# The choice of 256 keys in the 640-key block, moved from eight-at-a-time maxima to the shared bisection

## The chip, the cores and the metric

One core of a Trainium2 chip runs the whole kernel. The metric is the device time of one execution in microseconds (us). The engines are named as the profile names them: PE (TensorE's matrix products; PEld is its loading of weights), DVE (VectorE), ACT (ScalarE), POOL (GpSimd) and SP (SyncE, which issues the DMAs).

## What is computed

The kernel is one layer of a decoder over 1024 tokens of width 1024, in float32. Two token mixers work side by side on a common input projection: FoX, a causal softmax attention with a forget bias, and DSA, a sparse attention that lets each query see its 256 best keys only. Both have 8 heads of 64. Their outputs are gated, projected and normalised, and a SwiGLU block follows. The part that matters here is how DSA's keys are chosen, by an indexer's score:

```python
rel = jax.nn.relu(jnp.einsum('bqhd,bkd->bqhk', iqb, ik).astype(jnp.float32))
score = jnp.einsum('bqh,bqhk->bqk', iwb.astype(jnp.float32) * IDX_SCALE, rel)
score = jnp.where(kpos[None, None, :] <= qpos[None, :, None], score, NEG_INF)
_, idx = lax.top_k(score, topk)          # topk = 256
```

Queries come in blocks of 128. Block i may see 128*(i+1) keys, so blocks 0 and 1 need no choice, and blocks 2 to 7 choose 256 of 384, 512, 640, 768, 896 and 1024 keys.

## The kernel before

**Stages.** First the input is split into high and low parts (matrix products run as three products of such parts, `mm3`, lines 96 to 101), and the indexer's scores are made into six tiles `SM[2]` to `SM[7]`, [128 queries, 128*(i+1) keys] each (lines 242 to 284). Then comes the attention stage (lines 532 to 599): 64 steps, the first 32 for FoX and the last 32 for DSA. A step takes one head and one pair of query blocks, in the order of `ORDER = (3, 0, 2, 1)`. The mixing, the two normalisations and the feed-forward block follow, from line 600 on.

**One attention step.** `weigh` makes the scores of two query blocks on PE (lines 459 to 462). DVE takes the row maxima (line 469; for DSA's blocks with a choice line 472, which adds the mask `SM[i]` at the same time). ACT takes the exponentials (lines 470, 475), DVE the reciprocals (line 476), and POOL scales (line 479). `average` transposes the weights on PE (line 502), splits them on ACT and DVE (lines 503, 504) and multiplies with the values on PE (lines 511, 512). ACT and DVE put the result `o` together (lines 526, 527), which happens once in a step. Between these PE does `filler` work: projections for later heads, whose results ACT and DVE bring out of PSUM (lines 395, 396, 406, 407, 431, 432, 441), and gates (line 380).

**The choice of keys.** It is emitted at step `KSEL = 31` (lines 581 to 586), but its operands are ready much earlier. PE's order is written out by hand (`tc.manual_schedule`, line 564). A scheduler puts the instructions of the other engines in an order, and it draws the choice forward into FoX's steps. Once put in order, each engine works through its own list strictly in that order. There are two ways to choose:

- `select_by_max` (lines 287 to 292), on DVE alone: 32 times the eight greatest values are taken (`max`, line 290) and overwritten (`match_replace`, line 291); a last pass makes the mask (line 292). Before the change it serves the blocks of 384, 512 and 640 keys, one after the other.
- `select_by_bisection` (lines 294 to 361) finds the 256th greatest value bit by bit, for several blocks at once. In each of 32 counts ACT runs over every block's whole tile and counts by signs (line 310). DVE then makes of the counts, for all blocks together, the next bit and the next threshold in three tiny instructions (lines 311, 320, 318). ACT's next count waits for that threshold. After the loop DVE alone makes the last passes: two exact counts over each block (lines 333, 348), and for each piece of up to 512 keys a sequence of five passes that settles ties and writes the mask (lines 355 to 361). Before the change it serves the blocks of 768, 896 and 1024 keys.

```python
        def count(bias):
            for x, i in enumerate(blocks):
                j = at.tile([128, L], BF, name="junk", tag="junk", bufs=1)
                act.activation(j[:, :128 * (i + 1)], SM[i], AF.Sign, bias=bias(x), accum_out=s[:, x:x + 1])
            dve.tensor_tensor(a, s, thr, op=OP.is_ge)
```

The mask tiles are first read by DSA's steps (line 472).

Of the kernel before, what the change touches and what calls it, by code (L numbers as in the profile page):

```python
# [31 lines left out]
LAG = 2  # L32
W = (1, 1, 1, 1)
PW = 512
BIS = ((7, 6, 5),)
IDX_SCALE = (8 ** -0.5) * (64 ** -0.5)

NMM, NT = 2, 2
# [11 lines left out]
def trunk_kernel(ctx: ExitStack, tc: tile.TileContext, xT, xn, wt, wbr, wout, wfi, wfo,  # L50
# [236 lines left out]
    def select_by_max(i):  # L287
        for _ in range(TOPK // 8):
            m8 = mk.tile([128, 8], F32, name="m8", tag="m8", bufs=2)
            dve.max(m8, SM[i])  # L290
            dve.match_replace(SM[i], m8, SM[i], SENT)
        dve.tensor_scalar(SM[i], SM[i], SENT, -BIG, op0=OP.not_equal, op1=OP.mult)
# [280 lines left out]
    for k, (n, a, G) in enumerate(todo):  # L573
# [7 lines left out]
        if k == KSEL:  # L581
            for blocks in BIS:
                select_by_bisection(blocks, blocks[0])
            for i in range(2, 8):
                if not any(i in blocks for blocks in BIS):
                    select_by_max(i)
# [476 lines left out]
```

## Time and profile before

| | |
|---|---|
| median of 3 runs | 1687.06 us (1686.71 to 1687.7) |
| the profiled execution, its own time | 1685.55 us |
| the profiled execution, its span | 1683.6 us |
| PE busy | 1611.2 us, 96% of the span |
| PEld busy | 1314.1 us, 78% |
| DVE busy | 1186.1 us, 70% |
| ACT busy | 777.3 us, 46% |
| POOL busy | 673.3 us, 40% |

The span is the time from the first to the last instruction in the trace of the profiled execution; 1.95 us of its time lie around it. Busy times are those of one engine over the whole span. They are averages over stages of a very different kind, so what a change in one stage is worth has to be read from that stage: from the busy time of each engine in a stretch, and from what the waits in it end on.

### The profile page before, as it was taken

What the parts mean: (1) busy time and instruction counts of PE and PEld (TensorE: products, weight loads), DVE (VectorE), ACT (ScalarE), POOL (GpSimd) and SP (SyncE); (2) the same over time, 40 slices, a digit from 0 to 9 for tenths busy, and PEclk for the clock granted to TensorE, in tenths of its full rate; (3) what the DMA queues carried; (4) which work ended last, traced back from release to release, by engine and by line L of the source; (5) the groups of instructions that cost most, each with busy time, mean ns of one, the idle gap of its engine ahead of it and who ended that gap; (6) DMA issues with size and microseconds to landing.
All of it is one profiled execution on the core that took longest, in us unless ns stands there. A gap on an engine that the chain in (4) does not pass through costs nothing. (4 is left out here: it accounts for less than half of the span.)

```text
span 1683.6 us, 22519 instructions
## 1 busy us (share of the span) xinstructions
PE 1611.2 (96%) x7722; PEld 1314.1 (78%) x7722; DVE 1186.1 (70%) x2074; ACT 777.3 (46%) x1374; POOL 673.3 (40%) x652
## 2 busy tenths in 40 slices
PE   7998999998999999999999999999899999999997
PEld 5776887776788888888778877877677888888886
DVE  5889999979645454544775569776778766567776
ACT  6777878884444445544431034222123333253341
POOL 1122333332333333332441136434345555377673
PEclk9999999999999999999999999999899999999999
DMA  5112212121122222223865123565554333398552
GB/s 176 48 40 65 60 45 59 57 70 43 57 66 63 70 58 71 61 65 126 270 208 194 50 88 102 190 203 184 172 180 139 107 101 107 132 329 309 179 169 105
DMA packets 96379, 202.83 MB, mean 120 GB/s; under 512 B 10820, under 2 KB 37444, under 8 KB 96264
## 3 DMA queue, kind: packets, MB, share of 16 engines
q1 hardware_dynamic: 96264, 201.39, 36.6%
q8 instruction: 61, 1.00, 0.3%
q14 instruction: 54, 0.44, 0.1%
HBM read 139.40 MB, written 53.03 MB: 114 GB/s over the span
## 5 line engine op out<-in xcount | busy, mean ns | idle before, releaser
L99 PE MATMUL mm<-xh,whi 128*128 128x512 f32 (+1 forms) x720 | 296.0, 411 | 16.2 <-ACT whi L147 6.4
L101 PE MATMUL mm<-xl,whi 128*128 128x512 f32 (+1 forms) x720 | 281.4, 391 | 1.1 <-DVE xl L157 1.0
L100 PE MATMUL mm<-xh,wlo 128*128 128x512 f32 (+1 forms) x720 | 280.7, 390 | 0.5 <-DVE wlo L148 0.5
L479 POOL TENSOR_SCALAR p<-p,st 128x512 f32<-128x512 f32 (+1 forms) x192 | 113.8, 601 | 321.5 <-DVE st L476 268.8
L790 POOL TENSOR_TENSOR w<-ss,w 128x512 fp32r<-128x512 f32 x88 | 129.4, 1487 | 207.5 <-ACT w L789 188.8
L93 POOL TENSOR_TENSOR wlo<-wraw,whi 128x1024 fp32r<-128x1024 f32 x43 | 103.5, 2406 | 164.4 <-ACT whi L92 143.1
L99 PEld LDWEIGHTS mm<-xh,whi 128*128 128x128 f32 x720 | 136.8, 190 | 31.1 <-issue 6.4
L101 PEld LDWEIGHTS mm<-xl,whi 128*128 128x128 f32 x720 | 136.0, 189 | 32.0 <-DVE xl L157 2.3
L100 PEld LDWEIGHTS mm<-xh,wlo 128*128 128x128 f32 x720 | 136.8, 190 | 12.8 <-DVE wlo L148 1.0
L504 DVE TENSOR_TENSOR pl<-T,ph 128x512 fp32r<-128x512 f32 (+1 forms) x160 | 100.6, 634 | 36.6 <-ACT ph L503 34.7
L100 PE MATMUL acc<-fs 128*128 128x512 f32 x308 | 120.0, 389 | 0.6 <-DVE fs L930 0.6
L101 PE MATMUL acc<-fs 128*128 128x512 f32 x308 | 119.9, 389 | 0.0
L99 PE MATMUL acc<-fs 128*128 128x512 f32 x308 | 119.8, 389 | 0.0
L503 ACT ACTIVATE ph<-T 128x512 fp32r<-128x512 f32 (+1 forms) x160 | 87.3, 552 | 38.8 <-PE T L502 36.1
L310 ACT ACTIVATE junk<-sm,nt 128x1024 bf16<-128x1024 f32 (+2 forms) x93 | 96.8, 1041 | 14.6 <-DVE nt L318 12.8
L502 PE MATMUL T<-identf,p 128*128 128x128 f32 x576 | 90.6, 273 | 4.1 <-POOL p L479 2.0
L931 POOL TENSOR_TENSOR fs<-fraw,fs 128x512 fp32r<-128x512 f32 x47 | 81.1, 1740 | 26.9 <-ACT fs L929 23.1
L502 PEld LDWEIGHTS T<-identf,p 128*128 128x128 f32 x576 | 71.2, 140 | 26.1 <-DVE pl L504 4.1
L512 PE MATMUL O<-pl,V 128*128 128x256 f32 x320 | 82.3, 281 | 1.3 <-DVE pl L504 1.3
L511 PE MATMUL O<-ph,V 128*128 128x256 f32 x320 | 83.3, 282 | 0.0
L99 PE MATMUL pb<-x1h,w 128*128 128x512 f32 x176 | 72.0, 409 | 10.5 <-DVE h L858 9.3
L930 DVE TENSOR_TENSOR fs<-fraw,fs 128x512 fp32r<-128x512 f32 x47 | 57.0, 1225 | 31.1 <-ACT fs L929 31.1
(284 smaller groups left out, 4167.6 us busy)
## 6 DMA issues: line engine op xcount, KB each, us to landing
wraw<-in_wt_dram SPq DMA_DIRECT2D x45, 512.0 KB
fraw<-abd SPq DMA_DIRECT2D x30, 512.0 KB
wraw<-in_wfi_dram SPq DMA_DIRECT2D x25, 512.0 KB
wup<-in_wfi_dram SPq DMA_DIRECT2D x22, 512.0 KB
wb<-in_wfo_dram SPq DMA_DIRECT2D x44, 256.0 KB
abd<-wb SPq DMA_DIRECT2D x88, 128.0 KB
abd<-h SPq DMA_DIRECT2D x44, 256.0 KB
abd<-u SPq DMA_DIRECT2D x33, 256.0 KB
```

Of the source, the lines that this page charges most:

```text
L93: pool.tensor_tensor(lo, raw, f(hi), op=OP.subtract)
L99: te.matmul(ps, ah, bh, start=(first and i == 0), stop=False)
L100: te.matmul(ps, al, bh, start=False, stop=False)
L101: te.matmul(ps, ah, bl, start=False, stop=(last and i == n - 1))
L310: act.activation(j[:, :128 * (i + 1)], SM[i], AF.Sign, bias=bias(x), accum_out=s[:, x:x + 1])
L479: pool.tensor_scalar(pc, pc, st[:, 3:4], 1.0, op0=OP.mult, op1=OP.mult)
L502: te.transpose(T[:, s * 128:s * 128 + 128], P[qq][:, j * 128:j * 128 + 128], identf)
L503: act.activation(ph[:, c:], T[:, c:], AF.Copy)
L504: dve.tensor_tensor(pl[:, c:], T[:, c:], f(ph[:, c:]), op=OP.subtract)
L511: te.matmul(O, V[:, j, :], ph[:, r0:r0 + 256], start=(j == 0), stop=False)
L512: te.matmul(O, V[:, j, :], pl[:, r0:r0 + 256], start=False, stop=(last and jj == 1))
L790: pool.tensor_tensor(s[:, 1], raw, f(s[:, 0]), op=OP.subtract)
```

## The change

One constant is changed. Block 4, with its 640 keys, goes from `select_by_max` to the bisection, which now serves four blocks at once:

```diff
@@ -32,7 +32,7 @@
 LAG = 2
 W = (1, 1, 1, 1)
 PW = 512
-BIS = ((7, 6, 5),)
+BIS = ((7, 6, 5, 4),)
 IDX_SCALE = (8 ** -0.5) * (64 ** -0.5)
```

All else follows from lines 581 to 586: `select_by_max` is run for blocks 2 and 3 only, `count` has a fourth pass, the small tiles become four columns wide, and the last passes serve a fourth block. PE's list has the same instructions in the same order as before. On POOL a few clearings (lines 496, 497) change places with scalings next to them, and on SP a few loads and stores stand one or two places earlier or later. The lists of ACT and DVE change from the first count to the last pass. Three places follow. In the names, `sm_191` to `sm_196` are the tiles of the blocks of 384, 512, 640, 768, 896 and 1024 keys, `nt` is the threshold and `s` the counts.

On ACT, in FoX's later steps, from one output `o` on, before the change:

```order
L526 ACTIVATE o<-O 64x256
L380 ACTIVATE g<-mm 128x512
L310 ACTIVATE junk,s_4458<-sm_196,nt_4453 128x1024
L310 ACTIVATE junk,s_4458<-sm_195,nt_4453 128x896
L470 ACTIVATE p,st<-S,st 128x384
L503 ACTIVATE ph<-T 128x512 x2
L310 ACTIVATE junk,s_4458<-sm_194,nt_4453 128x768
L470 ACTIVATE p,st<-S,st 128x512
```

The same place with the change:

```order
L526 ACTIVATE o<-O 64x256
L380 ACTIVATE g<-mm 128x512
L310 ACTIVATE junk,s_4458<-sm_196,nt_4453 128x1024
L310 ACTIVATE junk,s_4458<-sm_195,nt_4453 128x896
L470 ACTIVATE p,st<-S,st 128x384
L503 ACTIVATE ph<-T 128x512
L310 ACTIVATE junk,s_4458<-sm_194,nt_4453 128x768
L503 ACTIVATE ph<-T 128x512
L310 ACTIVATE junk,s_4458<-sm_193,nt_4453 128x640
L470 ACTIVATE p,st<-S,st 128x512
```

The count over 640 keys stands as a fourth behind the other three, ahead of an exponential of the running step. A step later the change has this, on ACT:

```order
L470 ACTIVATE p,st<-S,st 128x1024
L526 ACTIVATE o<-O 64x256
L310 ACTIVATE junk,s_4458<-sm_193,nt_4453 128x640
L310 ACTIVATE junk,s_4458<-sm_196,nt_4453 128x1024
L470 ACTIVATE p,st<-S,st 128x128
```

Here the first count of an iteration stands directly behind the last one of the iteration before, with nothing between them. With the change there are five such places, before it none: at least one instruction always stood between.

On DVE, in FoX's steps with the third of the maxima, before the change:

```order
L290 MAX m_5070<-sm_193 128x8
L504 TENSOR_TENSOR pl<-T,ph 128x512 x2
L469 TENSOR_REDUCE st<-S 128x1
L318 SCALAR_TENSOR_TENSOR nt_4453<-u_4451,mp_4452 128x3
L291 MATCH_REPLACE sm_193<-m_5070,sm_193 128x640
L476 RECIPROCAL st<-st 128x1
L290 MAX m_5073<-sm_193 128x8
L504 TENSOR_TENSOR pl<-T,ph 128x512
L291 MATCH_REPLACE sm_193<-m_5073,sm_193 128x640
L290 MAX m_5076<-sm_193 128x8
L504 TENSOR_TENSOR pl<-T,ph 128x384
```

With the change, in the same steps:

```order
L504 TENSOR_TENSOR pl<-T,ph 128x512
L311 TENSOR_TENSOR a_4454<-s_4458,thr_4459 128x4
L320 SCALAR_TENSOR_TENSOR u_4451<-a_4454,u_4451 128x4
L318 SCALAR_TENSOR_TENSOR nt_4453<-u_4451,mp_4452 128x4
L476 RECIPROCAL st<-st 128x1
L504 TENSOR_TENSOR pl<-T,ph 128x512
L504 TENSOR_TENSOR pl<-T,ph 128x384
```

The maxima are gone from between the rows of the step, and the three tiny instructions of the bisection stand together. The maxima of the blocks of 384 and 512 keys keep their place ahead of this one.

On DVE, at the start of the last passes, before the change:

```order
L330 TENSOR_TENSOR v_4456<-u_4455,mp_4452 128x3
L333 TENSOR_SCALAR junk,s_4458<-sm_196,v_4456 128x1024
L469 TENSOR_REDUCE st<-S 128x1
L333 TENSOR_SCALAR junk,s_4458<-sm_195,v_4456 128x896
L333 TENSOR_SCALAR junk,s_4458<-sm_194,v_4456 128x768
```

With the change:

```order
L330 TENSOR_TENSOR v_4456<-u_4455,mp_4452 128x4
L333 TENSOR_SCALAR junk,s_4458<-sm_196,v_4456 128x1024
L333 TENSOR_SCALAR junk,s_4458<-sm_195,v_4456 128x896
L527 TENSOR_TENSOR o<-O,o 64x256
L333 TENSOR_SCALAR junk,s_4458<-sm_194,v_4456 128x768
L469 TENSOR_REDUCE st<-S 128x1
L333 TENSOR_SCALAR junk,s_4458<-sm_193,v_4456 128x640
```

The row maximum of the running step (line 469) now stands behind three of the exact counts in place of one. The whole of the last passes begins about one step later than before, and is longer by a fourth block.

## Rows read from the trace of the kernel before

**Rows 1.** Busy times by stretch: start:end, its length, each engine's busy time, PEclk, DMA
```profile
112.00:260.00 148.00, 141.72 (x752) 114.59 (x750) 144.47 (x362) 117.64 (x237) 48.02 (x71) 1.00 0.22 60
260.00:380.00 120.00, 114.82 (x628) 93.17 (x629) 106.20 (x245) 99.31 (x201) 38.99 (x66) 1.00 0.21 60
360.00:380.00 20.00, 19.64 (x104) 15.79 (x103) 10.70 (x28) 18.11 (x37) 6.36 (x10) 1.00 0.24 61
380.00:440.00 60.00, 52.67 (x272) 41.48 (x272) 54.56 (x108) 26.59 (x55) 19.00 (x26) 0.97 0.15 50
440.00:780.00 340.00, 340.00 (x1869) 288.29 (x1869) 160.56 (x391) 168.33 (x346) 117.36 (x190) 1.00 0.22 64
```

**Rows 2.** Waits of PE from 112 to 440 us: in total, times, longest
```profile
PE S L459 <- ACT p L470: 5.7, 8, 2.1
PE mm L99 <- DVE a L311: 2.2, 2, 1.5
```

**Rows 3.** DVE's groups by shape: busy us, mean ns, idle before; timeline: the first replacement
```profile
L290 DVE MAX8 m<-sm 128x8 f32<-128x640 f32 x32 | 26.1, 816 | 0.1
L291 DVE MATCH_REPLACE8 sm<-m,sm 128x640 f32<-128x640 f32 x32 | 25.8, 807 | 0.0
...
258.89 0.80 DVE L291 MATCH_REPLACE8 sm<-m,sm 128x640 f32<-128x640 f32 x1
```

**Rows 4.** Groups of ACT's counts, each shape apart, from 115 to 440 us
```profile
L310 ACT ACTIVATE junk<-sm,nt 128x1024 bf16<-128x1024 f32 x31 | 35.6, 1147 | 13.8 <-DVE nt L318 12.8 <-DVE mp L329 0.9
...
L310 ACT ACTIVATE junk<-sm,nt 128x768 bf16<-128x768 f32 x31 | 29.0, 934 | 0.4
```

**Rows 5.** Busy times of line 310 alone by stretch: ACT's time and instructions, two a pass
```profile
112.00:260.00 148.00, 56.78 (x101) 1.00 0.22 60
260.00:380.00 120.00, 48.29 (x86) 1.00 0.21 60
```

**Rows 6.** Groups of DVE's last passes, each shape apart, and line 361's own shortest/median/longest
```profile
L333 DVE TENSOR_SCALAR_CACHE_REDUCE junk<-sm,v 128x768 bf16<-128x768 f32 x1 | 1.0, 1012 | 0.0
...
L356 DVE TENSOR_TENSOR_SCAN cum<-e 128x512 f32<-128x512 bf16 x4 | 4.9, 1218 | 0.0
...
L360 DVE SCALAR_TENSOR_TENSOR sm<-sm,k,e 128x512 f32<-128x512 f32 x4 | 3.0, 749 | 0.0
L357 DVE SCALAR_TENSOR_TENSOR e<-cum,s,e 128x512 bf16<-128x512 f32 x4 | 3.0, 747 | 0.1
...
L361 DVE TENSOR_SCALAR sm<-sm x6: 420/514/2657, 406.0 to 430.8; 128x512 f32<-128x512 f32 x4, 128x384 f32<-128x384 f32 x1, 128x256 f32<-128x256 f32 x1
```

**Rows 7.** Timeline: start us, duration us, of DVE rows that lasted long, and POOL beside them
```profile
127.84 2.39 POOL L93 TENSOR_TENSOR wlo<-wraw,whi 128x1024 fp32r<-128x1024 f32 x1 [9.58 <-ACT whi L92]
128.09 2.15 DVE L320 SCALAR_TENSOR_TENSOR u<-a,u 128x3 int32<-128x3 int32 x1
...
387.59 2.32 DVE L330 TENSOR_TENSOR v<-u,mp 128x3 int32<-128x3 int32 x1
...
410.35 2.29 DVE L361 TENSOR_SCALAR sm<-sm 128x512 f32<-128x512 f32 x1
```

**Rows 8.** Timeline of PE: the two longest gaps of the last passes, in brackets
```profile
386.24 0.47 PE L99 MATMUL mm<-xh,whi 128*128 128x512 f32 x1 [2.04 <-DVE V L432]
...
414.80 0.45 PE L459 MATMUL S<-K,Q 128*128 128x384 f32 x1 [2.05 <-ACT p L470]
```

**Rows 9.** Busy times in the stretch behind the first of these gaps; PEclk is third from last
```profile
385.00:391.00 6.00, 4.76 (x17) 3.63 (x17) 5.57 (x14) 2.45 (x6) 2.74 (x3) 0.72 0.02 5
```

**Rows 10.** Timeline of ACT: a count directly behind the one before it
```profile
378.67 0.19 ACT L310 ACTIVATION_READ_ACCUMULATOR junk<-sm,nt 128x1 f32 x1
...
380.15 1.15 ACT L310 ACTIVATE junk<-sm,nt 128x1024 bf16<-128x1024 f32 x1 [0.89 <-DVE mp L329]
```

**Rows 11.** Timeline of DVE: the choice's last pass, and the first reader of a mask
```profile
430.76 2.66 DVE L361 TENSOR_SCALAR sm<-sm 128x256 f32<-128x256 f32 x1
...
474.67 1.09 DVE L472 CUSTOM_DVE_ANT_0 p<-S,sm 128x896 f32<-128x896 f32 x1 [1.48 <-PE S L462]
```

## The prediction

> **What bounds the kernel now.** I first read the busy time of each engine by stretch, for the time in which the keys are chosen [rows 1]. From 440 to 780 us, in DSA's steps, PE is busy in all of 340.00 us and nothing else matters: whatever FoX's steps lose or save is handed on one to one. Before that PE has gaps. It is idle for 148 - 141.72 = 6.28 us from 112 to 260 us, for 5.18 us from 260 to 380 and for 7.33 us from 380 to 440, together 18.8 us. PE's list is the same with the change, so these gaps, and those that may be added, are what is at stake. In the first two stretches DVE is busy for 144.47 of 148 and 106.20 of 120 us, ACT for 117.64 and 99.31. In the last one DVE is busy for 54.56 of 60 and ACT for 26.59 only.
>
> Next, PE's waits [rows 2]: the dearest end on ACT's exponential (line 470), which itself follows DVE's row maximum, and others on DVE's tiny bisection rows. No single operation is at fault. The reader is to see two in-order lists, both well filled, in which a row of the step stands behind rows of the choice.
>
> Matmul busy time hides small losses between pipelined products. The Trainium skill (Trainium Kernel Development and Optimization, Performance Expectations) says to judge by LDWEIGHTS busy share instead. By that, the 249.2 us of PEld work from 112 to 440 us at the 84.8% of DSA's steps would take 294 us of the 328, so 34 us would be at stake, not 18.8. The rows speak partly against it: from 360 to 380 us PE was idle for 0.36 us, and PEld still stood at 79% only, so most of that difference is FoX's other mix of products [rows 1]. I keep 18.8 us.
>
> **The change, part by part.**
>
> *Removed from DVE:* 32 steps of a maximum, 816 ns, and a replacement, 807 ns [rows 3], 51.9 us in all, a little less where neighbours overlap. They are the third of the three selections on DVE; the first replacement starts at 258.89 us [rows 3], so they lie in the second stretch. There DVE falls from 106.2 to some 55 us, 46%. The first stretch keeps its maxima of 384 and 512 keys, and DVE stays as full as it is.
>
> *Added on ACT:* 32 passes over 640 keys. Line 310 took 56.78 us for 101 instructions, two a pass, so 1.12 us a pass at a mean of 896 keys [rows 5]. A key costs (1147 - 934) / 256 = 0.83 ns [rows 4], so 640 keys cost 1.12 - 0.21 = 0.91 us, and all 32 passes 29 us. By the instructions of [rows 5] 16.8 counts lie in the first stretch and 14.3 in the second. ACT rises to 117.64 + 15.3 = 133 us (90%) in the first and 99.31 + 13.0 = 112 us (94%) in the second. The tiny rows go from three to four columns, which I cost at nothing.
>
> *Added on DVE, in the last passes:* two exact counts, each between 640/768 of 1012 ns and all of it, 1.7 to 2.0 us; a piece of 512 keys, 1218 + 747 + 749 + two at 514 = 3.7 us [rows 6], where I price line 355 like line 361, the same form; a piece of 128 keys, between a quarter and a half of that, 0.9 to 1.9 us, taken as 1.4. The sum is 6.9 us (6.4 to 7.7). Today's last passes run from 387.59 [rows 7] to 433.42 us [rows 11], 45.8 us, so they grow by 15%.
>
> *Moved:* on POOL and SP only neighbours change places; I cost that at nothing, since POOL was busy for 38.99 of 120 us [rows 1].
>
> What this is worth on PE, by stretch:
>
> 1. From 112 to 260 us DVE's load stays and ACT's grows. A gain is excluded, as nothing leaves. From above: ACT's free time is halved (30 to 15 us), and if the idle time doubles with it the price is 6.3 us. I take +1.0, near the lower end, because ACT still has a tenth of its time free.
> 2. From 260 to 380 us the engine that was full becomes half empty, and the other nearly full. One row shows just that mix: from 360 to 380 us, with the maxima over, DVE was busy for 54% and ACT for 91%, and PE idled 0.36 us in 20 [rows 1]. At that rate 120 us lose 2.2 us in place of 5.18: -3.0. The ends are -5.2, if all of it goes, and +5.4 (first rival).
> 3. From 380 to 440 us the last passes hold the step up for 15% longer: 7.33 x 0.15 = +1.1. On the other side, today's longest gap there, 2.04 us [rows 8], begins while the last iteration's list is being worked off; then line 330, a tiny instruction, lasts 2.32 us beside a POOL instruction [rows 7], and the granted clock falls to 0.72 for 6 us [rows 9], some 1.7 us more. With other neighbours this may not meet again. I take half of 3.7 us, -1.9, together -0.8. The ends are -4.7 (both long gaps of [rows 8] and the slow clock gone, the extra length kept) and +4, if the new length makes two more gaps of 2 us.
>
> A rule to weigh: three DVE rows lasted over 2 us each where others of their kind take a fraction of it, and a POOL instruction of 2.39 us ran beside the first [rows 7]. The Trainium skill (SBUF — State Buffer, Who interferes with whom) says that a DVE instruction with two SBUF inputs, or in a two-port mode, is held for the whole of a GpSimd instruction that holds the shared port pair, and that others are not. It speaks against this change: the removed maxima have one input and cannot be held, the added last passes can. Line 361 was held in two of six rows [rows 6, 7], so two more of them would give 0.67 more holds, each with a gap of some 2 us behind it; by the rule the sum below would be 1.4 us worse, 1685.7. Since the page's mechanism also covers what may fall away in line 330, I leave the sum as it is.
>
> The sum is 1.0 - 3.0 - 0.8 = -2.8 us. Against the profiled execution's 1685.55 us (its span and 1.95 us around it) that is 1682.8 us. The median of the runs is 1687.06 us, 1.5 us above it, so **1684.3 us** for the median.
>
> **The rivals.**
>
> *ACT becomes the bound (slower).* In the second stretch ACT would have 120 - 112.3 = 7.7 us free. ACT's wait for the threshold took 12.8 us in all [rows 4], about half of it here, 6.4 us. And at the five places where the first count now stands directly behind the last one, ACT can only wait for DVE: from the end of a count at 378.86 to the next at 380.15 that took 1.3 us [rows 10], so 6.5 us in five places. Together 12.9 us, 5.2 to 5.4 us more than is free. The point from which it decides is a wait of over 7.7 us. With the +1.0 of the first stretch and nothing saved in the third it gives +6.4, 1693.5 us. For it: exponentials and splits that PE needs stand behind counts in one list. Against it: with DVE half empty the threshold should come at once, and some of the 1.3 us was another row's work.
>
> *The gaps go altogether (faster).* If a free DVE answers every row at once, the second stretch saves 4.9 of its 5.18 us and the third 4.7: -9.6 us, 1677.5 us. For it: PE's waits are behind rows of DVE, directly or by way of the exponential [rows 2]. Against it: they exist in the first stretch at the same DVE load, and ACT now fills up.
>
> *Wait for wait.* Each gap that DVE no longer makes is made by ACT: 1687.1 us. The first and the third stretch already hold most of the gaps, and neither is relieved.
>
> *The mask comes too late, so that the work isn't hidden.* The last pass ends at 433.42 us, the first reader starts at 474.67 [rows 11]: 41.3 us. If nothing overlapped, the loop would take 29 us longer and the last passes 6.9, 36 us. It just fits, so this has 0.02; each us over would cost one.
>
> **How the numbers follow.** The measurement of this kernel can tell some 0.2%, 3.4 us, from no change. The forecast has 0.52. Its own spread is about 4 us either way, so it holds 0.20 of faster, 0.30 of no change and 0.02 of slower. ACT as the bound has 0.20 (slower), gaps gone 0.20 (faster), wait for wait 0.06 (no change), the late mask 0.02 (slower). That makes faster 0.40, no change 0.36, slower 0.24. The range goes from the fast rival's 1677.5 to the slow one's 1693.5 us, which leaves out half of each, 0.2 in all. Cases of both signs hold much of the chance; the forecast's own range is 1680 to 1688.5 us.
>
> **What the profile would show.** If I am right: PE idle near 2 us in the second stretch, 7 in the first and 6 to 7 around the last passes; ACT over 90% and DVE near half in the second; passes over 640 keys at 0.9 us; the last passes over 50 us long, one step later; DSA's steps full as before. If ACT waits for the threshold for over 8 us from 260 us on and PE's waits there end on ACT, the first rival is right. The prediction is wrong in kind if the first stretch changes by more than 6 us, or if a stage behind 440 us changes its length.

## The result, and the profile after

On the chip of this comparison the kernel before takes 1687.16 us (median of 6 runs, 1686.71 to 1689.74) and the changed one 1678.12 us (median of 6, 1677.22 to 1679.8). The ratio is 0.9946, with a 95% interval of 0.9936 to 0.9956: **9.0 us faster**, where 2.8 were forecast. The profiled execution of the changed kernel took 1679.8 us (span 1678.0).

The busy times of the changed kernel by stretch, in the columns of [rows 1]:

```profile
112.00:260.00 148.00, 144.32 (x762) 116.25 (x761) 141.78 (x361) 129.24 (x264) 49.10 (x74) 1.00 0.22 64
260.00:380.00 120.00, 118.78 (x656) 97.37 (x655) 62.52 (x153) 114.35 (x239) 38.97 (x66) 1.00 0.20 57
360.00:380.00 20.00, 20.00 (x109) 16.31 (x109) 10.61 (x28) 19.79 (x42) 6.73 (x11) 1.00 0.24 61
380.00:440.00 60.00, 53.42 (x291) 42.80 (x291) 52.32 (x119) 30.67 (x67) 21.60 (x27) 1.00 0.17 55
440.00:780.00 340.00, 338.63 (x1856) 287.08 (x1855) 166.06 (x406) 167.80 (x344) 118.09 (x191) 1.00 0.22 64
```

PE's idle time, the length of a stretch less PE's busy time in it, against the forecast:

| stretch, us | before | after | difference | forecast |
|---|---|---|---|---|
| 112 to 260 | 6.28 | 3.68 | -2.60 | +1.0 |
| 260 to 380 | 5.18 | 1.22 | -3.96 | -3.0 |
| 380 to 440 | 7.33 | 6.58 | -0.75 | -0.8, the clock included |
| 440 to 780 | 0.00 | 1.37 | +1.37 | 0 |

These add up to -5.9 us. PE's clock adds to them: from 380 to 440 us the granted clock is 1.00 where it was 0.97, and the 0.72 of [rows 9], worth 1.7 us, does not come back. With it the third stretch stands at -2.5 us where -0.8 was forecast, so the near agreement in that row of the table is none.

PE's waits from 112 to 440 us (in total, times, longest), where those of [rows 2] were 5.7 and 2.2:

```profile
PE T L502 <- POOL p L479: 5.4, 4, 2.8
PE S L459 <- ACT p L470: 3.0, 4, 2.0
...
PE mm L99 <- DVE a L311: 0.7, 2, 0.5
```

ACT's counts by shape (busy us, mean ns | idle before). ACT waits for the threshold for 8.0 us, less than the 12.8 of [rows 4], though it is busy for 95% of the second stretch:

```profile
L310 ACT ACTIVATE junk<-sm,nt 128x1024 bf16<-128x1024 f32 x31 | 35.6, 1147 | 8.1 <-DVE nt L318 8.0
...
L310 ACT ACTIVATE junk<-sm,nt 128x640 bf16<-128x640 f32 x31 | 25.8, 831 | 0.5
```

The largest surprise is the first stretch, from which no instruction was taken. The timeline of the kernel before, around its first gaps (start us, duration us; in brackets the idle time before, and what ended it). The first and last rows bound the stretch that is called the steps below:

```profile
107.17 1.57 POOL L283 TENSOR_SCALAR_AFFINE_SELECT sm<-sm 128x128 f32<-128x128 f32 x2 [10.26 <-DVE sm L279]
...
131.40 0.69 DVE L407 TENSOR_TENSOR K<-mm,K 64x512 fp32r<-64x512 f32 x1
...
132.24 0.47 PE L99 MATMUL mm<-xh,whi 128*128 128x512 f32 x1 [1.73 <-DVE K L407]
...
141.92 2.40 POOL L93 TENSOR_TENSOR wlo<-wraw,whi 128x1024 fp32r<-128x1024 f32 x1 [11.69 <-ACT whi L92]
142.88 1.45 DVE L318 SCALAR_TENSOR_TENSOR nt<-u,mp 128x3 int32<-128x3 int32 x1
...
149.76 0.47 PE L99 MATMUL mm<-xh,whi 128*128 128x512 f32 x1 [1.48 <-DVE a L311]
...
577.31 0.38 ACT L526 ACTIVATE o<-O 64x256 f32<-64x256 f32 x1 [2.96 <-PE O L512]
```

The same of the changed kernel:

```profile
108.02 1.57 POOL L283 TENSOR_SCALAR_AFFINE_SELECT sm<-sm 128x128 f32<-128x128 f32 x2 [10.25 <-DVE sm L279]
...
129.07 2.40 POOL L93 TENSOR_TENSOR wlo<-wraw,whi 128x1024 fp32r<-128x1024 f32 x1 [9.95 <-ACT whi L92]
129.77 0.56 DVE L290 MAX8 m<-sm 128x8 f32<-128x384 f32 x1
...
131.86 0.47 PE L99 MATMUL mm<-xh,whi 128*128 128x512 f32 x1 [0.49 <-DVE a L311]
132.17 0.14 DVE L320 SCALAR_TENSOR_TENSOR u<-a,u 128x4 int32<-128x4 int32 x1
...
394.33 0.17 DVE L330 TENSOR_TENSOR v<-u,mp 128x4 int32<-128x4 int32 x1
...
409.19 0.55 PE L502 MATMUL T<-identf,p 128*128 128x128 f32 x3 [2.78 <-POOL p L479]
417.61 2.51 POOL L93 TENSOR_TENSOR wlo<-wraw,whi 128x1024 fp32r<-128x1024 f32 x1 [0.40 <-ACT whi L92]
417.91 3.29 DVE L356 TENSOR_TENSOR_SCAN cum<-e 128x512 f32<-128x512 bf16 x1
426.08 0.50 PE L459 MATMUL S<-K,Q 128*128 128x512 f32 x1 [1.96 <-ACT p L470]
...
448.12 0.23 DVE L361 TENSOR_SCALAR sm<-sm 128x128 f32<-128x128 f32 x1
...
467.44 1.09 DVE L472 CUSTOM_DVE_ANT_0 p<-S,sm 128x896 f32<-128x896 f32 x1 [1.48 <-PE S L462]
...
570.08 0.38 ACT L526 ACTIVATE o<-O 64x256 f32<-64x256 f32 x1 [2.96 <-PE O L512]
```

Before, the tiny row of line 320 came just after POOL's subtraction (line 93) had begun, and was held to its end [rows 7]. Line 407, by which PE gets its next PSUM buffer, stood behind it in DVE's list, and PE idled for 1.73 us. Now each count has a fourth pass, so line 320 comes some 4 us later. Beside POOL's row stand maxima, with one input from SBUF, and they take 0.56 us as always. Where a DVE row is held up beside such a row of POOL, I call it a **meeting**. The change has meetings of its own, among them line 356, which waits out POOL's row at 417.61 us and takes 3.29 us. And its last passes, from 394.33 to 448.35 us, bring gaps of 2.78 and 1.96 us, as the last passes before did (2.05 us, [rows 8]).

A second measure takes the later stages out of it, which took 1105.8 to 1109.1 us in the profiled executions of this study: **the steps**, from POOL's first clearing of line 283 to ACT's 41st output of line 526. Before they took 577.31 - 107.17 = 470.14 us, now 570.08 - 108.02 = 462.06: -8.1 us. The rest of the 9.0 us is within what the other stages vary by.

### The profile page after: what moved, and what is told of

It is laid out like the page before. It is cut to its first block, busy times and chain, and to the rows that moved or that the text cites. A ratio compares the mean times of both kernels' runs of the same rounds, so it can differ in the third digit from the quotient of the medians.

```text
span 1678.0 us, 22488 instructions
## 1 busy us (share of the span) xinstructions
PE 1604.1 (96%) x7722; PEld 1309.0 (78%) x7722; DVE 1135.5 (68%) x1994; ACT 801.5 (48%) x1438; POOL 673.9 (40%) x652
## 5 line engine op out<-in xcount | busy, mean ns | idle before, releaser
L100 PEld LDWEIGHTS mm<-xh,wlo 128*128 128x128 f32 x720 | 136.8, 190 | 12.8 <-DVE wlo L148 1.0
L310 ACT ACTIVATE junk<-sm,nt 128x1024 bf16<-128x1024 f32 (+1 forms) x124 | 122.6, 989 | 9.2 <-DVE nt L318 8.0
```

Of the source, the lines that this page charges most:

```text
L100: te.matmul(ps, al, bh, start=False, stop=False)
```

## The experiments

| kernel | median, us | ratio to before, 95% interval | the steps, us against before | PE's idle time in the steps, us | at half clock in the steps, us |
|---|---|---|---|---|---|
| before | - | - | - | 18.8 | 3.4 |
| the change | 1678.12 | 0.9946 [0.9936, 0.9956] | -8.1 | 12.9 | 0 |
| order of the blocks reversed | 1685.24 | 0.9996 [0.9987, 1.0005] | -0.8 | 16.6 | 6.8 |
| the maxima of 640 keys left out | 1682.32 | 0.9976 [0.9965, 0.9986] | -3.4 | 13.9 | 10.2 |
| a fourth pass added, maxima kept | 1680.37 | 0.9964 [0.9950, 0.9977] | -5.8 | 12.2 | 3.4 |
| five blocks by bisection | 1686.54 | 1.0002 [0.9993, 1.0011] | +0.2 | 18.4 | 3.4 |
| the change without block 4's last passes | 1677.06 | 0.9950 [0.9936, 0.9964] | -9.9 | 11.6 | 0 |
| before, POOL's row in 4 pieces | 1673.21 | 0.9925 [0.9912, 0.9938] | -8.0 | 12.0 | 3.4 |
| the change, 4 pieces | 1673.15 | 0.9928 [0.9915, 0.9941] | -8.2 | 12.0 | 3.4 |
| fourth pass, 4 pieces | 1675.48 | 0.9940 [0.9928, 0.9953] | -6.7 | 12.5 | 0 |
| before, 2 pieces | 1678.07 | 0.9953 [0.9941, 0.9966] | -4.9 | 15.4 | 0 |
| maxima left out, 4 pieces | 1675.59 | 0.9936 [0.9922, 0.9950] | -7.4 | 12.9 | 3.4 |
| before, 8 pieces | 1672.22 | 0.9922 [0.9909, 0.9934] | -8.4 | 10.0 | 6.8 |
| the change, 8 pieces | 1672.03 | 0.9923 [0.9909, 0.9936] | -9.8 | 10.5 | 3.4 |

The last three columns come from one profiled execution of each kernel. In every one the granted clock stood at 1.00 for nearly all of the steps; the last column says for how long it stood at half (1.2 in place of 2.4 GHz). That differs from kernel to kernel, each 3.4 us of it can cost up to 1.7 us, and no run shows how it varies between executions of one kernel. So differences of 1 to 2 us in the steps are not read as effects below.

### The parts of the change, one at a time

**The same work in another order.**

```diff
-BIS = ((7, 6, 5),)
+BIS = ((5, 6, 7),)
```

> The kernel before with its three bisected blocks named in the other order (5, 6, 7): the same instructions, other places in the lists of ACT and DVE. Theory 1 (the maxima that left DVE made the gain): no change, 1687 +- 1.5 us. Theory 2 (the gain is mostly that long waits of single DVE rows beside POOL no longer met, which any other order could bring): 1679 to 1684 us, or as far above 1687.

1685.24 us, no change. This other order of the passes within a count does not give the gain. It tests theory 2 less than I meant it to, since it left the first two meetings where they were: line 320 takes 2.16 us at 127.94 us, and line 318 takes 1.43 us at 142.74.

**DVE's relief alone.**

```diff
-        for _ in range(TOPK // 8):
+        for _ in range(TOPK // 8 if i < 4 else 0):
```

> The kernel before, with the 32 steps of maxima for the 640-key block left out and nothing put in their place (its mask is then wrong: the choice in that block is left out). The relief of DVE alone. Theory 1 (DVE's relief is the gain, ACT's 29 us cost next to nothing): 1676 to 1678 us, the same as the change or up to 2 us faster, since the fourth block's last passes are missing too. Theory 3 (the relief is worth more, and ACT's added passes take part of it back): 1670 to 1674 us. Theory 2 (order): anything, with a gain that does not go with the gaps of the second stretch.

1682.32 us: less than half of the gain in time. So DVE's relief isn't the whole of it. PE's idle time in the steps fell by 4.9 us, though, nearly as much as with the change (5.9), while the time at half clock rose from 3.4 to 10.2 us and took a part of it back; whether that goes with this kernel or with this one execution, no run shows.

**ACT's added work alone.**

```diff
-        nb = len(blocks)
+        nb = len(blocks) + 1
...
+        dve.memset(thr[:, 3:4], 0.0)
...
-            for x, i in enumerate(blocks):
+            for x, i in enumerate((*blocks, 4)):
...
-                act.activation(j[:, :128 * (i + 1)], SM[i], AF.Sign, bias=bias(x), accum_out=s[:, x:x + 1])
+                act.activation(j[:, :128 * (i + 1)], SM[max(i, 5)][:, :128 * (i + 1)], AF.Sign, bias=bias(x), accum_out=s[:, x:x + 1])
```

> The kernel before with a fourth pass of 640 keys in every count (over a tile that is ready, its result unused), the maxima kept and no last passes added. ACT's load alone, with DVE still full. Theory 1: 1687 to 1689 us, as ACT has the time free. Theory 3: 1691 to 1695 us. ACT busy at 90% from 112 to 260 us in both.

1680.37 us. Pure additional work made the kernel 5.9 us faster, more than the relief did. In this run the gap of 1.73 us is one of 0.47, at 131.25 us, much as in the changed kernel (0.49). What ACT's added passes cost, if anything, is hidden in this; what they bring can only come from where the rows stand in the lists, and from when they run.

**Five blocks.**

```diff
-BIS = ((7, 6, 5),)
+BIS = ((7, 6, 5, 4, 3),)
```

> The change and one block more: the bisection also chooses for the 512-key block. DVE loses another 43.6 us of maxima, now in the first stretch, ACT gains 26 us. Theory 1 without a limit: a further gain of 3 to 5 us, 1673 to 1675 us. Theory 3 (ACT's list becomes the bound, the first rival of the prediction): ACT over 95% busy from 112 to 420 us and the time at or above the change's, 1678 to 1690 us; and the last passes end at DSA's first reader of a mask, which may add some us.

1686.54 us, no change, but for two opposite reasons. By the 28th output this kernel was 12.4 us ahead of before (1.3 of them from ahead of the steps); by the 32nd 0.9 us was left. ACT was not the bound: it was busy for 284.8 of the 308 us from 112 to 420, 92%. DVE's timeline shows last passes still at work when the first masks are read, and the busy times from 440 to 490 us show PE idle for 8.1 us, where before it had no idle time:

```profile
469.38 0.34 DVE L361 TENSOR_SCALAR sm<-sm 128x384 f32<-128x384 f32 x1
471.29 1.06 DVE L472 CUSTOM_DVE_ANT_0 p<-S,sm 128x896 f32<-128x896 f32 x1
...
479.20 1.35 DVE L361 TENSOR_SCALAR sm<-sm 128x256 f32<-128x256 f32 x1
...
440.00:490.00 50.00, 41.94 (x221) 32.90 (x220) 49.59 (x103) 19.02 (x40) 15.54 (x18) 1.00 0.19 56
```

### The long POOL row

The meetings can be tested without touching the choice: cut the row that DVE meets. A piece then holds a DVE row only for its own length.

**The kernel before, four pieces.**

```diff
-        pool.tensor_tensor(lo, raw, f(hi), op=OP.subtract)
+        [pool.tensor_tensor(lo[:, x:x + 256], raw[:, x:x + 256], f(hi)[:, x:x + 256], op=OP.subtract) for x in range(0, 1024, 256)]
```

> The kernel before, with POOL's subtraction for the low weight halves (line 93) in four pieces of 256 columns in place of one of 1024. Theory of meetings: PE's long gaps come from DVE rows that are held as long as that POOL row runs (2.15 us beside 2.39), and the change gains because its longer count loop sets those rows elsewhere. Then no DVE row is held over 0.8 us here, the gaps of 1.73 us at 132 and 2.04 us at 386 us shrink below 0.7, the clock stays at full after 385 us, and the time falls by 4 to 8 us, to 1679 to 1683. Theory of pace: a fourth pass lets the step's rows go ahead on ACT, whatever POOL does. Then the gaps stay and the time is that of the kernel before within 1.5 us. Theory of load: DVE's 52 us of maxima are the cause; the time is that of before.

1673.21 us: 13.3 us faster than before, more than expected, and faster than the change. The busy times by stretch, and one short stretch:

```profile
112.00:260.00 148.00, 144.59 (x770) 117.51 (x769) 144.09 (x373) 120.23 (x245) 52.91 (x101) 0.99 0.23 64
260.00:380.00 120.00, 115.90 (x634) 94.27 (x633) 102.99 (x246) 100.72 (x203) 42.43 (x86) 1.00 0.20 56
380.00:440.00 60.00, 55.48 (x303) 44.52 (x302) 49.61 (x102) 26.03 (x54) 22.46 (x41) 1.00 0.20 60
...
375.00:381.00 6.00, 4.78 (x26) 3.89 (x26) 5.57 (x17) 2.62 (x7) 3.17 (x6) 1.00 0.01 3
```

Its timeline:

```profile
123.48 2.82 POOL L93 TENSOR_TENSOR wlo<-wraw,whi 128x256 fp32r<-128x256 f32 x4 [9.12 <-ACT whi L92]
...
134.98 0.50 PE L99 MATMUL mm<-xh,whi 128*128 128x512 f32 x1 [1.57 <-ACT vT L441]
...
376.22 0.47 PE L99 MATMUL mm<-xh,whi 128*128 128x512 f32 x1 [2.03 <-DVE V L432]
...
401.97 0.44 PE L459 MATMUL S<-K,Q 128*128 128x384 f32 x1 [0.89 <-ACT p L470]
```

The edit is a clean one: in the two traces the rows of PE, DVE and ACT are the same and start in the same order, and so are POOL's but for the pieces. (The same holds for every pair of kernels with and without pieces here.) So the gaps of this kernel can be laid against those of before, one by one. The gap of 1.58 us at 140.95 us is still there (1.57, at 134.98), and so is that of 2.04 at 386.24 [rows 8] (2.03, at 376.22); I had expected the latter to go, wrongly. Gone or smaller are those that follow a held row:

| held row before, start and us | gap behind it, us | with four pieces |
|---|---|---|
| L320, 128.09, 2.15 | 1.73 at 132.24 | none |
| L318, 142.88, 1.45 | 1.48 at 149.76 | none |
| L292, 256.41, 2.50 | 1.32 at 261.27 | none |
| L318, 316.81, 1.81 | 0.69 at 329.04 | none |
| L361, 410.35, 2.29 | 2.05 at 414.80 | 0.89 |

That is 1.73 + 1.48 + 1.32 + 0.69 + 1.16 = 6.4 us of the 8.0 us by which the steps are shorter. PE's idle time in them falls by 6.8 us; the remaining 1.2 us is not put down to single rows. (Two more held rows, line 330 with 2.32 us [rows 7] and line 361 with 2.66 us [rows 11], have no gap behind them.)

The clock is not part of this sum. Before, it was at half from 386.6 us on, 1 us before line 330 began, and with pieces it was at half for as long at another place, behind the gap of 1.57 us. The busy times of these two stretches, before and with pieces:

```profile
386.60:390.00 3.40, 3.40 (x10) 2.40 (x9) 3.23 (x10) 0.85 (x1) 2.36 (x1) 0.50 0.02 5
...
135.80:139.20 3.40, 3.40 (x10) 2.62 (x9) 3.33 (x9) 2.24 (x5) 3.25 (x5) 0.50 0.01 2
```

Another 4.3 us come from the stage ahead of the steps (line 283 begins at 102.83 in place of 107.17 us), where line 279 had met the same row (2.47 us at 76.64, 2.50 us at 95.36). That PE simply gets its low weight halves sooner is no explanation: from 0 to 440 us it waits for them once, for 0.5 us, in both kernels, and the four pieces take longer than the one row did (2.82 against 2.39 us).

**The change, four pieces** (the diff of the change and the line above).

> The change with the same four pieces on POOL. Theory of meetings: the change has three holds left in the steps (0.99, 1.29 and 3.29 us), with one gap of 2 us behind the last of them, so it gains less by the pieces than the kernel before does: 1 to 3 us, to 1675 to 1677; and the change's lead over the kernel with pieces falls from 9 us to some 3 to 5. Theory of pace: the change's lead over the kernel with pieces stays at 8 to 10 us.

```profile
112.00:260.00 148.00, 143.90 (x767) 115.92 (x766) 138.94 (x361) 130.81 (x270) 52.81 (x101) 1.00 0.23 64
260.00:380.00 120.00, 119.47 (x661) 98.20 (x660) 62.65 (x151) 114.68 (x239) 44.05 (x88) 1.00 0.21 58
380.00:440.00 60.00, 52.63 (x281) 42.34 (x280) 55.17 (x120) 27.16 (x58) 23.58 (x38) 0.97 0.20 64
```

1673.15 us, the same as the kernel before with pieces, within some 2 us by the intervals. The lead of 9 us is gone: it was not cut to 3 to 5 us, as the theory of meetings had it, but to nothing that can be told. In the steps the change gained nearly nothing by pieces (-8.1 to -8.2): PE's idle time fell by 0.9 us, and the clock was at half for 3.4 us where it had not been before. Against the kernel before with pieces PE's idle time moves by +0.7, -3.6 and +2.9 us in the three stretches.

**Both parts again, with four pieces** (the diffs of the fourth pass and of the maxima left out, each with the line above).

> The kernel before with the four pieces on POOL, and with the fourth pass of 640 keys in every count (its sum is thrown away, the maxima stay, no last passes are added). Without the pieces that pass brought 5.9 us. Theory of meetings: that gain came from DVE rows that no longer met the long POOL row; with no long POOL row it is gone, and the time is that of the kernel with pieces, 1673.2 us, within 2 us, or a little above it, as ACT has 29 us more to do. Theory of pace: the pass lets the steps go ahead by itself, and the time falls by another 4 to 6 us, to 1667 to 1669.

> The kernel before with the four pieces, and the 32 maxima and replacements of the block of 640 keys left out, with nothing in their place. The relief of DVE alone, without the long POOL rows: the change less this relief should be what the added last passes and ACT's passes cost. By PE's idle time in the two kernels with pieces (4.10 and 0.53 us in the second stretch) it is worth 3 to 4 us, 1669 to 1670.5 us. If a free DVE brings nothing by itself, 1673 us.

1675.48 and 1675.59 us. The fourth pass, worth -5.9 us with the long POOL row, brings nothing without it, and neither does the relief, worth -3.9 us with it. By the medians they are 2.3 and 2.4 us slower than the kernel before with pieces, by the steps 1.3 and 0.6 us; the intervals overlap, so that they cost something is not shown. The expectation for the relief fell, since it took DVE's relief to be worth something by itself. PE's gaps did not go away with the maxima: the last passes begin with line 330 at 355.45 us in place of 377.57, and bring their gaps into the second stretch.

One gap goes by pace, whatever POOL does. PE's list is the same in all these kernels, so a gap can be followed from one to another. The gap of 2.04 us [rows 8] is 2.02 to 2.40 us in every kernel with three passes in a count, with the maxima or without, with pieces or without; in every kernel with four passes it is 0.41 us or less, and with five it is 2.36 again. The maxima left out, and the fourth pass with four pieces (its line 433 is line 432 of the kernel before):

```profile
390.02 0.47 PE L99 MATMUL mm<-xh,whi 128*128 128x512 f32 x1 [2.37 <-DVE V L432]
...
376.64 0.47 PE L99 MATMUL mm<-xh,whi 128*128 128x512 f32 x1 [0.40 <-DVE V L433]
```

The kernels with four passes have other gaps in its place, in the change 2.78 us at 409.19 and 1.96 at 426.08 us.

**Two pieces and eight.** The same line with 512 and with 128 columns.

> The kernel before with POOL's subtraction in two pieces of 512 columns. If the time lost is the length for which a DVE row is held, a hold is at most half as long (1.2 us) and the time lies between that of before and that with four pieces, near 1678 to 1680 us. If a shift of the lists decides by luck, it can lie anywhere from 1673 to 1687 us, and the stage ahead of the steps, which has no choice of keys in it, would still give back a part of its 4.3 us, 2 to 3 us.

> The kernel before with POOL's subtraction in eight pieces of 128 columns. One piece, two and four gave 1686.2, 1678.1 and 1673.2 us. If the time goes on following the length of the longest hold, which halves from about 0.6 us, it gains another 1 to 3 us, 1670.5 to 1672.5 us. If holds of 0.6 us already cost nothing, 1673 us; if POOL's own row gets so long that something waits for the low halves, over 1674 us.

> The change with the eight pieces. With four, the change and the kernel before gave the same time. Theory of meetings: they stay within 2 us of each other, since neither has holds that matter. If the change has a gain of its own that four pieces hid by chance, it leads by 3 us or more.

1678.07, 1672.22 and 1672.03 us. With two pieces the first held row is about half as long; DVE's timeline:

```profile
125.69 1.04 DVE L320 SCALAR_TENSOR_TENSOR u<-a,u 128x3 int32<-128x3 int32 x1
```

So the time of the kernel before follows the length of the hold: 1686, 1678, 1673, 1672 us for one piece, two, four, eight. From four on nothing is left to win that can be told (ratios to before of 0.9925 and 0.9922), and with eight the change and the kernel before are again level. Both kernels, with four or with eight pieces, beat both kernels of this study.

**The change without its added last passes.**

```diff
-        for x, i in enumerate(blocks):
+        for x, i in enumerate(blocks[:3]):
```

> The change, with the passes of lines 345 to 361 left out for the block of 640 keys (its mask stays unmade); its count at line 333 and all 32 passes on ACT stay. This takes away what the prediction priced at +1.1 us of PE time and what the starts of ACT's last rows of a step suggest costs up to 5.7 us between 385 and 450 us. If the added last passes hold PE up in proportion to their length, 1677 us, 1 below the change. If the last stretch's gaps are mostly theirs, 1673 to 1675 us. If the gaps there come from where DVE's rows are held beside POOL, no change beyond 1 us either way, since the pieces only shift.

1677.06 us. The ratio cannot be told from the change's. The median is 1.1 us lower, and in the profiled executions the steps are 1.8 us shorter, so the added last passes cost some 2 us at most, not the 5.7 us that the starts of the steps had suggested.

## Why the prediction was right and wrong

The direction was right and the time lies in the range, 6.2 us under the forecast and near the figure of the rival by which the gaps go altogether (1677.5). But it was not that rival: PE still idles for 12.9 us of its 18.8. That the range held is in part luck, as its lower end came from a rival that did not come about, and most of the gain from a cause that the sum did not have.

**The first stretch is the step that failed.** It said "A gain is excluded, as nothing leaves", and took +1.0. Measured: -2.6. A gap can go without any work leaving, when the rows of a list shift in time against another engine's. Both rows of the first meeting were in the prediction [rows 7], but I used them to weigh a rule and not to price the gap behind them. The Trainium skill (SBUF — State Buffer, Who interferes with whom) says that a DVE instruction with two SBUF inputs, or in a two-port mode, waits for a GpSimd instruction that has the shared port pair, and one with a single SBUF input outside those modes does not. This trace agrees on both sides: line 320 was held for 2.15 of POOL's 2.39 us, and the maxima beside POOL's row took 0.56 us as elsewhere. The mechanism was right, and the sign I gave it wrong: I weighed the holds of added rows (+1.4 us, left out of the sum), and of the rows whose hold the new pace could undo only line 330.

**The second stretch**: -3.0 forecast, -4.0 measured, and -3.6 between the two kernels with pieces. The size was right, the reason only in part: two of the gaps that went, 1.32 and 0.69 us, stood behind held rows, and the pieces alone remove them too. Nor was it a gain of the whole: with pieces the third stretch gives back 2.9 us of it in other gaps, and the first 0.7.

**The third stretch**: the gap of 2.04 us and the slow clock are gone in full (I took half of 3.7 us). But I had the clock fall with line 330 beside POOL, and it had fallen 1 us before that row began. And the gap goes with the fourth pass: with pieces alone it stays. The added length cost some 2 us at most, as the run without these passes shows; +1.1 was forecast. They run from 394.33 to 448.35 us, 54.0 us, as forecast (52.7), a step later, and so past the end of my stretch, where another 1.37 us was lost.

**The rivals.** ACT did come to 129.24 and 114.35 us of busy time (133 and 112 were forecast), but it did not become the bound: its wait for the threshold fell, and PE idles 1.22 us there. The last pass ends 19 us ahead of the first reader (448.35 against 467.44 us), so the mask is in time; with five blocks it is not. "Wait for wait" is what the change is worth without the long POOL row: 0.1 us with four pieces, 0.2 with eight, neither of which can be told from nothing.

## What to carry to other kernels

Where two engines hold each other up, list the rows that lasted many times their usual time, look for the gap behind each, and price it, before any edit: here the gaps behind five such rows shrank by 6.4 us when the row that they met was cut, and the steps by 8.0. Any edit that shifts one of the two lists undoes some of these meetings and makes others, so a part of its result is luck. Take the long partner away first, here by cutting one POOL row into four, and only then judge the edit; and where additional work alone brings a gain, look for a meeting that it has undone.

## What was not expected of the hardware

Cutting POOL's subtraction costs little: 2.39 us for one row of 1024 columns, 2.82 for four pieces, 3.41 for eight:

```profile
122.87 3.41 POOL L93 TENSOR_TENSOR wlo<-wraw,whi 128x128 fp32r<-128x128 f32 x8 [8.55 <-ACT whi L92]
```

PE's clock did not follow the gap alone. Before, a gap of 2.04 us and 4.76 us of work in 6 went with a granted clock of 0.72 [rows 8, 9]; with four pieces a gap of 2.03 us and 4.78 us of work in 6 went with 1.00, and there it was the gap of 1.57 us at 134.98 that the half clock followed, while behind the 1.58 us of before it stayed at 1.00. What makes the difference stays open.
